# An S5 recurrence rewritten as a real scan in a turning frame, and a pause ahead of the scores of cached keys

## The chip, the core and the metric

The kernel runs on one core of a Trainium2 chip. The metric is the time of one execution in device microseconds. The engines are named as the profile names them: PE (TensorE; PEld is its loading of weights), DVE (VectorE), ACT (ScalarE), POOL (GpSimd) and SP (SyncE, which here issues nearly all DMAs). Each engine works through its own instructions strictly in the order in which they were written; a semaphore wait of one instruction holds all behind it on that engine.

## The reference

One inference step of a two-layer trunk for two groups of positions that share weights: a prompt of 256 frames and a running stream ("sample") of 32 frames with 512 cached keys. The width is 2048. Layer 0 is attention: 8 heads with a forget bias and 8 "differential" heads (two softmax maps each). Layer 1 is a diagonal complex state-space layer (S5): 128 groups of 16 channels with 64 complex states each. Cut to what the change touches:

```
# differential heads; k is the cached keys followed by the new ones
s = q @ k.T * scale + bias            # bias = -slope * distance
p = softmax(s1) - lam * softmax(s2)
# S5: abar = exp(dt * a), complex, one value for each (group, state)
bu      = einsum(u, bbar)             # complex input of each state
x[t]    = abar * x[t-1] + bu[t]       # x[-1] is zero (prompt) or the stream's state (sample)
y[t]    = Re(c @ x[t]) + d * u[t]
```

The outputs are the new residual streams of both groups, new cache rows, and the final states of both groups.

## The kernel before

All 288 positions (256 + 32) are processed at once, with features on the partitions. The weights stream from memory as tiles `w` of 1 MB through four slots (`wst`). Each quarter of a tile (128x512) is split into a rounded part `hi` (a CAST on ACT) and a rest `lo` (a subtraction on DVE), since one matmul takes reduced-precision operands; the activations are split likewise into `ah` and `al`. A 128x128 block of weights then costs three matmuls into `m`: `ah,hi`, `al,hi`, `ah,lo`. There are 8 `hi`/`lo` buffers (NQ). These m matmuls are the main stream, and a "job" of the main stream is 48 of them.

All else is side work, written as Python generators (`Tasks`): attention heads, the adaLN modulation (`mod_ps`), discretisation (`disc`), and the S5 stage. A planner (`Plan`) keeps a modelled clock for each engine while the program is built: a cost for every instruction, a "written" and "read" time for every region of a tile. After each main-stream block `Tasks.step` lets a side task go on when the planner's PE time has passed `plan.last`, the end of what that task last wrote; the words that a task yields (`"next dve"`, `"next soon"`, `"act"`) say which engine's backlog may hold it. So the order on all five engines is fixed at build time, out of estimated costs. Every engine call goes through the wrapper `Engine`, hence line L116 for all instructions in the profile: one goes by tile names.

`diff_sample(b, ck)` computes the sample group's scores of a pair of differential heads: it loads the bias `bi`, and then multiplies queries with the cached keys `CK` (`ck`, loaded by DMA CK<-in_kdT) into `Ss`, and with the new keys into `Ss2`.

In the S5 stage the position axis is cut into blocks of LC = 8; the state is carried from block to block, so there are JP = 32 steps for the prompt and 4 for the sample (NJ = 36; NX = 38 columns with the two starting states). The side tasks of the stage:
- `state_in` takes the four 512-wide groups of u (16 feature tiles, four at a time). When a group is done on the main stream it is written to memory (ud<-MX) and gathered back in another layout (MX<-ud, eight small DMAs). Matmuls `xin_ps` (16 units xin1 to xin16, four for a group of u) give the block inputs, and ACT copies them into X.
- `scan(g0)` runs the recurrence over blocks for 16 of the 64 group pairs at once, four times in all, one for each group of u. Before, it is a loop over the 32 steps, of four small instructions at first (prompt and sample together) and of three later (prompt alone), all on DVE, with tiles `t` and `rot`, the matrix of the eighth power of abar.
- `slices` (16 units y1 to y16): ACT copies the states into `Xm`, matmuls with a loaded tile `v` give `y_ps`, ACT copies them into `Yg`, and each four of them go to memory (yd<-Yg, eight small DMAs). The v tiles come through a ring of three.
- `inside` (16 units t1 to t16): the part within a block, matmuls t_ps with tiles `kb`.
- the gelus load yd back (yx<-yd), add it to MX on DVE, and take the ACT function (yx<-MX).

The four groups of u end after 192, 384, 576 and 768 m matmuls of this stage (counted from its first); the gates z follow.

Of the kernel before, what the change touches and what calls it, by code (L numbers as in the profile page):

```python
# [8 lines left out]
F32 = mybir.dt.float32  # L9
# [15 lines left out]
NJ = T // LC  # L25
# [70 lines left out]
class Engine:  # L96
# [38 lines left out]
    def cost(self, fn, out, ins, outs, k):  # L135
        p = self.plan
        n = 1
        for d in out.shape[1:]:
            n *= d
        if fn == "dma_start":  # L140
            t = max([p.when(p.written, a) for a in ins] + [p.at[self.name], p.base.get(out.tensor.name, 0.0)])
            p.at[self.name] = t + (0.45 if self.name != "pool" else 1.0)
            size = self.pieces(out, ins[0])
            if self.name == "act":
                end = t + 3.2 + 2 * size
            else:
                p.at["dma"] = max(p.at["dma"], t + 1.2) + size
                end = p.at["dma"] + 2.0
            p.note(p.written, out, end)
            for a in ins:  # L150
                p.note(p.read, a, end)
            p.last = max(p.last, end)
            return
        if self.name == "pe":
            r = ins[1] if len(ins) > 1 else ins[0]
            w = 1
            for d in r.shape[1:]:
                w *= d
            m = out.shape[0]
            c = 0.107 if fn != "matmul" else w * 0.00042 + 0.01 if r.dtype == F32R else max(w * 0.00042, 0.024) if m <= 32 \  # L160
                else max(w * 0.00168, m * 0.00167)
            c += 0.003
        elif self.name == "act":
            c = n * 0.000833 + 0.1 + (0.1 if len(outs) > 1 else 0)
        elif self.name == "dve":
            if fn == "tensor_reduce":
                n = ins[0].shape[1] * (ins[0].shape[2] if len(ins[0].shape) > 2 else 1)
            c = 0.07 + n * (0.0063 if fn == "reciprocal" else 0.00055 if fn in ("tensor_copy", "memset") or fn == "tensor_scalar" and len(ins) < 2 else 0.00105)
# [103 lines left out]
def build(tc, I, O):  # L272
# [8 lines left out]
    with ExitStack() as ctx:  # L281
# [23 lines left out]
        def TT(o, a, b, op, eng=dve):  # L305
            eng.tensor_tensor(o, a, b, op=op)
# [401 lines left out]
        def disc(V, rot, spt):  # L708
# [29 lines left out]
            yield  # L738
            TT(apr[:, :, 1], mg, s2, ALU.mult)
            TT(api[:, :, 1], mg, s1, ALU.mult)  # L740
            yield "next"
            for k in range(2, 9):
                p, q = k // 2, k - k // 2
# [4 lines left out]
                TT(s2, api[:, :, p], apr[:, :, q], ALU.mult)  # L748
                TT(api[:, :, k], s1, s2, ALU.add)
                yield "next"  # L750
            dve.tensor_copy(rot[:, :, 0:4:3], apr[:, :, 8:9].to_broadcast([128, 64, 2]))
            tsc(rot[:, :, 1], api[:, :, 8], -1.0)
            dve.tensor_copy(rot[:, :, 2], api[:, :, 8])
            TT(s1, ar, ar, ALU.mult)
            TT(s2, ai, ai, ALU.mult)
            TT(s1, s1, s2, ALU.add)
# [530 lines left out]
        def diff_sample(b, ck):  # L1287
            q, k = qkv["qd", b], qkv["kd", b]
            bi = sc.tile([128, PAST + TS], F32, tag="bias_s", name="bi")
            sp.dma_start(bi, I["biasS"][b])  # L1290
            nm = sc.tile([128, 2], F32, tag="nms", name="nms")
            sm = sc.tile([128, 2], F32, tag="sms", name="sms")
            zz = [sc.tile([128, PAST + TS], F32, tag="zs%d" % m, name="zs") for m in range(2)]
            for m in range(2):
                yield from room(2)
                S, S2 = take([128, PAST], "Ss"), take([128, TS], "Ss2")
                sample_scores(S, S2, q, k, ck, slice(64 * m, 64 * m + 64))
                if m:
# [24 lines left out]
            yield from sample_out(zz[0], "d", b, cv, scale)  # L1323
# [143 lines left out]
        rot1 = sp1.tile([128, 64, 4], F32, name="rot1")  # L1467
        sp.dma_start(rot1, rot_d)
        SZ = sp1.tile([128, KT, T], F32, name="SZ")
        X = sp1.tile([128, 64, 2, NX], F32, name="X")  # L1470
        dT = pload("dT", (128, KT))
        hbglu = pload("bgluT", (128, KT))
        tsc(hbglu, hbglu, 0.5)
# [111 lines left out]
        def state_in():  # L1585

            w1_ahead(0)
            for i in range(KT):
# [21 lines left out]
                x = X[:, 4 * i:4 * i + 4]  # L1610
# [8 lines left out]
            ready.add("w1_read")  # L1619
            yield  # L1620

        def scan(g0):
            n = 16
            Xh = X[:, g0:g0 + n]
            rot = rot1[:, g0:g0 + n, :]
            dve.memset(Xh[:, :, :, 0:1], 0.0)
            dve.tensor_copy(Xh[:, :, :, JP + 1], sfin[:, 1, g0:g0 + n, :])
            for j in range(JP):
                if j < NJ - JP:
                    cur = Xh[:, :, :, j:j + JP + 2:JP + 1]  # L1630
                    nxt = Xh[:, :, :, j + 1:j + JP + 3:JP + 1]
                    t = [sl.tile([128, n, 2, 2], F32, tag="t%d" % i, name="t") for i in range(2)]
                    TT(t[0], cur, rot[:, :, 0:1].unsqueeze(3).to_broadcast([128, n, 2, 2]), ALU.mult)
                    TT(t[1], cur[:, :, ::-1, :], rot[:, :, 1:3].unsqueeze(3).to_broadcast([128, n, 2, 2]), ALU.mult)
                    TT(nxt, nxt, t[0], ALU.add)
                    TT(nxt, nxt, t[1], ALU.add)
                else:
                    nxt = Xh[:, :, :, j + 1]
                    t = sl.tile([128, n, 2, 2], F32, tag="t%d" % (j % 2), name="t")
                    TT(t, Xh[:, :, :, j].unsqueeze(2).to_broadcast([128, n, 2, 2]),  # L1640
                       rot.rearrange("p g (o r) -> p g o r", o=2), ALU.mult)
                    TT(nxt, nxt, t[:, :, :, 0], ALU.add)
                    TT(nxt, nxt, t[:, :, :, 1], ALU.add)
                yield "next soon"
            dve.tensor_copy(sfin[:, 0, g0:g0 + n, :], Xh[:, :, :, JP])
            dve.tensor_copy(sfin[:, 1, g0:g0 + n, :], Xh[:, :, :, NX - 1])
# [6 lines left out]

        def v_load(i):
            if i < KT:
                vt[i] = sl.tile([128, 2, 4, 9, 16], F32, tag="v%d" % (i % 3), name="v2")
                sp.dma_start(vt[i].rearrange("p r g k c -> p r (g k c)"), v2_d[i])

        def kb_load(i):
# [4 lines left out]
        def slices():  # L1664

            Xm = sl.tile([128, 4, 2, 2, NX - 1], F32, name="Xm")
            pool.memset(Xm, 0.0)
            for i in range(3):
                v_load(i)
            for i in range(KT):  # L1670
                yield from wait(("x", i // 4))
# [1 line left out]
                if i % 4 == 0:  # L1673
                    Yg = sl.tile([128, 32, NJ], F32, tag="Yg", name="Yg")
                for e in range(2):
                    act.copy(Xm[64 * e:64 * e + 64, :, :, e, :], X[64 * e:64 * e + 64, 4 * i:4 * i + 4, :, 0:NX - 1])
                yield "act"
                yield from room()
                ps = take([128, 4, 2, NX - 1], "y_ps")
# [5 lines left out]
                act.copy(y[:, :, :, 0:JP], ps[:, :, :, 0:JP])  # L1685
                act.copy(y[:, :, :, JP:NJ], ps[:, :, :, JP + 1:NX - 1])
                give(ps)
                v_load(i + 3)
                if i % 4 == 3:
                    plan.last = plan.when(plan.written, Yg)  # L1690
                    yield "act"
# [133 lines left out]
        free = X.rearrange("p a r j -> p (a r j)")  # L1825
# [159 lines left out]
```

## Time and profile before

| | |
|---|---|
| runs shown | 1337.06 us median of 3 (1335.88 to 1342.54) |
| the profiled execution | 1335.96 us, of which its span is 1334.2 us |
| granted clock of TensorE, mean | 0.974 |
| PE busy | 1248.5 us, 94% |
| PEld, DVE, ACT busy | 1107.4, 922.8 and 593.8 us |
| DMA | 334.56 MB, mean 251 GB/s |

The columns of a timeline row are start (us), duration (us), engine, line, operation, tiles, shapes, count, and in brackets the idle time of the engine ahead of it with what ended it. A row of the windows has the stretch, its length, the busy time of PE, PEld, DVE, ACT and POOL with the number of instructions, then the granted clock (1.00 is full speed), the busy share of the DMA engines and the GB/s. A row of the waits has the engine and what it was about to do, what it waited for, the sum (us), the times and the longest.

### The profile page before, as it was taken

The numbers are of one execution on the slowest core, as the hardware profiler recorded it, in microseconds if no ns is written. First come the engines' busy times: TensorE is split into PE (matmuls) and PEld (weight loads), VectorE is DVE, ScalarE is ACT, GpSimd is POOL, SyncE is SP. The second block draws the span as 40 slices with busy tenths as digits, with TensorE's granted clock in tenths as the row PEclk, the third lists the DMA queues.
The fourth block names the chain that finished last, engine by engine and source line by source line (L and its number), as shares of the span: only waits on it lengthen the run. The fifth ranks groups of instructions, "written<-read, shape, count | busy, mean of one in ns | idle before, by whom it ended". The sixth has DMA issues, their size and how long they took to land.

```text
span 1334.2 us, 27951 instructions
## 1 busy us (share of the span) xinstructions
PE 1248.5 (94%) x11098; PEld 1107.4 (83%) x11098; DVE 922.8 (69%) x2210; ACT 593.8 (45%) x1394; POOL 31.1 (2%) x20
## 2 busy tenths in 40 slices
PE   5999899999999969999999999998879999999996
PEld 2798788888778858887889998897869999999895
DVE  5579987698887777887664873865749585455554
ACT  4534233344354524654643573242435684444441
POOL 0006000000000000000000000000000000000000
PEclk8999999999999979999999999998889999999998
DMA  9978687588989858988776396876657657677631
GB/s 356 370 294 335 225 306 260 190 296 336 323 284 356 310 201 290 324 302 311 275 253 228 133 362 168 195 220 176 161 162 187 189 184 267 236 273 269 228 123 71
DMA packets 114161, 334.56 MB, mean 251 GB/s; under 512 B 47696, under 2 KB 64096, under 8 KB 83312
## 3 DMA queue, kind: packets, MB, share of 16 engines
q1 hardware_dynamic: 101360, 303.14, 65.5%
q10 hardware_dynamic: 12672, 29.65, 6.1%
q8 instruction: 87, 1.43, 0.4%
q14 instruction: 42, 0.34, 0.1%
HBM read 297.69 MB, written 35.06 MB: 249 GB/s over the span
## 4 chain that ended last, share of the span: by engine, by line
issue 43%; PE 31%; DVE 12%; DMA 10%; ACT 3%; POOL 0%; ACTq 0%; SPq 0%; DVEq 0%; POOLq 0%
PE m L116 24%; DMA w<-in_w_in_att 4%; PE mod_ps L116 4%; DMA v_d<-v 3%; DVE lo L116 3%; DVE v L116 2%; DVE MX L116 1%; DMA w_d<-W 1%; DVE tmpv L116 1%; ACT hi L116 1%; DVE qkv L116 1%; DVE dtmp L116 1%; DVE ssq L116 1%; DMA CK<-in_kdT 1%; DVE al L116 1%
## 5 line engine op out<-in xcount | busy, mean ns | idle before, releaser
L116 PE MATMUL m<-ah,hi 128*128 128x288 f32 (+1 forms) x2304 | 712.6, 309 | 9.7 <-ACT hi L116 4.8
L116 PE MATMUL m<-ah,lo 128*128 128x288 f32 (+1 forms) x2304 | 686.5, 298 | 1.7 <-DVE lo L116 1.6
L116 PE MATMUL m<-al,hi 128*128 128x288 f32 (+1 forms) x2304 | 687.4, 298 | 0.0
L116 PEld LDWEIGHTS m<-ah,hi 128*128 128x128 f32 x2304 | 439.8, 191 | 69.5 <-issue 33.9
L116 ACT CAST hi<-w 128x512 fp32r<-128x512 f32 x552 | 322.5, 617 | 358.0 <-PE m L116 236.6
L116 DVE TENSOR_TENSOR lo<-w,hi 128x512 fp32r<-128x512 f32 x552 | 369.6, 687 | 144.9 <-ACT hi L116 142.4
L116 PEld LDWEIGHTS m<-ah,lo 128*128 128x128 f32 x2304 | 440.0, 191 | 3.1 <-DVE lo L116 3.0
L116 PEld LDWEIGHTS m<-al,hi 128*128 128x128 f32 x2304 | 440.4, 191 | 0.3
L116 PE MATMUL mod_ps<-w,cs 128*32 128x512 f32 x744 | 97.8, 620 | 12.6 <-DVE ssq L116 12.6
L116 DVE SCALAR_TENSOR_TENSOR qkv<-m,qkv 128x288 f32<-128x288 f32 x168 | 73.3, 454 | 26.0 <-PE m L116 25.8
L116 DVE TENSOR_TENSOR X<-X,t 128x32 f32<-128x32 f32 (+1 forms) x256 | 58.1, 227 | 8.3
L116 DVE TENSOR_TENSOR v<-pt,raw 128x512 f32<-128x512 f32 (+1 forms) x64 | 46.0, 719 | 22.1 <-DMA v_d<-v 18.8
L116 DVE SCALAR_TENSOR_TENSOR MX<-m,gate,MX 128x256 f32<-128x256 f32 x96 | 30.8, 363 | 31.2 <-PE m L116 31.1
L116 PEld LDWEIGHTS mod_ps<-w,cs 128*32 128x32 f32 x744 | 17.2, 110 | 38.2 <-issue 22.0
L116 PE MATMUL y_ps<-Xm,v 128*128 128x74 f32 x256 | 34.3, 292 | 13.0 <-ACT Xm L116 12.8
L116 DVE TENSOR_TENSOR tmpv<-pt,raw 128x512 f32<-128x512 f32 (+1 forms) x64 | 46.0, 718 | 0.0
L116 PEld LDWEIGHTS y_ps<-Xm,v 128*128 128x128 f32 x256 | 33.3, 209 | 13.9 <-ACT Xm L116 13.9
L116 ACT ACTIVATE yx<-MX 128x288 f32<-128x288 f32 (+1 forms) x38 | 18.8, 495 | 56.4 <-DVE MX L116 55.8
L116 PE MATMUL t_ps<-MX,kb 32*32 32x288 f32 (+7 forms) x1024 | 40.1, 306 | 2.8 <-DMA kb<-kb_d 2.8
L116 PEld LDWEIGHTS t_ps<-MX,kb 32*32 32x32 f32 x1024 | 28.7, 107 | 14.3 <-issue 4.4
L116 DVE SCALAR_TENSOR_TENSOR MX<-MX,c_dT,t_ps 128x288 f32<-128x288 f32 x16 | 8.2, 513 | 44.0 <-PE t_ps L116 44.0
L116 DVE TENSOR_TENSOR v<-v,tmpv 128x512 f32<-128x512 f32 (+1 forms) x48 | 34.3, 714 | 1.7
(225 smaller groups left out, 904.3 us busy)
## 6 DMA issues: line engine op xcount, KB each, us to landing
w<-in_w_mod SPq DMA_DIRECT2D x93, 1024.0 KB, 6.2
w<-in_w_in_att SPq DMA_DIRECT2D x40, 1024.0 KB, 7.7
w<-in_w_in_ssm SPq DMA_DIRECT2D x32, 1024.0 KB, 5.4
w<-in_w_wide SPq DMA_DIRECT2D x24, 1024.0 KB, 10.3
w<-in_w_out_att SPq DMA_DIRECT2D x16, 1024.0 KB, 6.9
w<-in_w_glu SPq DMA_DIRECT2D x14, 1024.0 KB, 5.1
w<-in_w_out_ssm SPq DMA_DIRECT2D x12, 1024.0 KB, 5.0
v_d<-v ACTq DMA_DIRECT2D x16, 576.0 KB, 7.8
```

What stands on the lines that cost most here:

```text
L116: return f(*a, **k)
```

## The change

Four things change.

1. Discretisation (`disc`): `rot` no longer holds the eighth power of abar as a matrix. It now holds the cosine and sine of eight times the angle (three rounds of angle doubling), and the eighth power of the magnitude. The planner gets a cost of its own for `tensor_tensor_scan`.
2. `diff_sample`: after its tiles are made, the task sets `plan.last` to the time at which the planner expects `ck` and `bi` to be there, and yields. So other work is put ahead of `Ss` until the planned PE time has reached that.
3. The S5 recurrence. A new task `turn_task` builds for each 16 group pairs the turns E[j] = (cos, sin) of j times the angle by doubling (w = 1, 2, 4, 8, 16: five rounds of four DVE instructions), and a table R of decays (an ACT copy). `scan` multiplies the inputs by the conjugate turn, runs the real and the imaginary part as one `tensor_tensor_scan` each (16 chains of 38 columns in a row, a decay of 0 at each start), and multiplies back. X gets the layout [part, group, column], so that a scan reads one contiguous row.
4. The ring of the v tiles has two slots in place of three (`v_load(i + 2)`).

The core of the diff:

```diff
@@ disc
+            for _ in range(3):
+                TT(n_, s1, s1, ALU.mult)
+                TT(th, s2, s1, ALU.mult)
+                TT(s2, s2, s2, ALU.mult)
+                TT(s2, s2, n_, ALU.subtract)
+                tsc(s1, th, 2.0)
+            dve.tensor_copy(rot[:, :, 0], s2)
+            dve.tensor_copy(rot[:, :, 1], s1)
+            TT(mg, mg, mg, ALU.mult)
+            TT(mg, mg, mg, ALU.mult)
+            TT(rot[:, :, 2], mg, mg, ALU.mult)
+            dve.memset(rot[:, :, 3:4], 0.0)
...
-            dve.tensor_copy(rot[:, :, 0:4:3], apr[:, :, 8:9].to_broadcast([128, 64, 2]))
-            tsc(rot[:, :, 1], api[:, :, 8], -1.0)
-            dve.tensor_copy(rot[:, :, 2], api[:, :, 8])
@@ diff_sample
+            plan.last = max(plan.when(plan.written, ck), plan.when(plan.written, bi))
+            yield
             for m in range(2):
                 yield from room(2)
@@ the S5 stage
-        X = sp1.tile([128, 64, 2, NX], F32, name="X")
+        X = sp1.tile([128, 2, 64, NX], F32, name="X")
...
+        def turn_task():
+            n = 16
+            for h in range(4):
+                yield from wait(*[("x", h - 1)] * (h > 0))
...
+                dve.tensor_copy(E[:, :, :, 1], rot[:, :, 0:2])
+                act.copy(R, rot[:, :, 2:3].to_broadcast([128, n, NX]))
+                dve.memset(R[:, :, 0:JP + 2:JP + 1], 0.0)
+                yield "next dve"
+                for w in (1, 2, 4, 8, 16):
...
+                    TT(t, a[:, :, ::-1, :], z, ALU.mult)
+                    TT(b, a, c, ALU.mult)
+                    TT(b[:, :, 0], b[:, :, 0], t[:, :, 0], ALU.subtract)
+                    TT(b[:, :, 1], b[:, :, 1], t[:, :, 1], ALU.add)
+                    yield "next dve"
+                dve.tensor_copy(E[:, :, :, JP + 1:NX], E[:, :, :, 0:NX - JP - 1])
@@ scan, inner part
-            for j in range(JP):
-                if j < NJ - JP:
...
-                    TT(t[0], cur, rot[:, :, 0:1].unsqueeze(3).to_broadcast([128, n, 2, 2]), ALU.mult)
-                    TT(t[1], cur[:, :, ::-1, :], rot[:, :, 1:3].unsqueeze(3).to_broadcast([128, n, 2, 2]), ALU.mult)
-                    TT(nxt, nxt, t[0], ALU.add)
-                    TT(nxt, nxt, t[1], ALU.add)
-                else:
...
-                yield "next soon"
+            for back in range(2):
+                for h in range(0, n, m):
...
+                    TT(t, Xh[:, ::-1], z, ALU.mult)
+                    TT(Xh, Xh, c, ALU.mult)
+                    yield "next soon"
+                    TT(Xh[:, 0], Xh[:, 0], t[:, 0], ALU.subtract if back else ALU.add)
+                    TT(Xh[:, 1], Xh[:, 1], t[:, 1], ALU.add if back else ALU.subtract)
+                    yield "next soon"
+                for ri in range(0 if back else 2):
+                    x = X[:, ri, g0:g0 + n, :].rearrange("p g j -> p (g j)")
+                    dve.tensor_tensor_scan(x, R.rearrange("p g j -> p (g j)"), x, 0.0, op0=ALU.mult, op1=ALU.add)
+                    yield "next soon"
@@ v ring
-                vt[i] = sl.tile([128, 2, 4, 9, 16], F32, tag="v%d" % (i % 3), name="v2")
+                vt[i] = sl.tile([128, 2, 4, 9, 16], F32, tag="v%d" % (i % 2), name="v2")
...
-                v_load(i + 3)
+                v_load(i + 2)
@@ start of the S5 stage
+        side.add(turn_task())
         side.add(state_in())
```

The order on the engines moves at many places. Three of them follow.

First, PE, at the first scores of the sample group's cached keys against the second pair of heads. Before:

```order
L116 MATMUL m<-ah,lo 128x288
L116 MATMUL S<-qkv 128x128
L116 MATMUL S<-qkv 128x256
L116 MATMUL Ss<-CK,MX 32x512 x4
L116 MATMUL Ss_5869<-qkv,MX 32x32 x4
L116 MATMUL m<-ah,hi 128x288
```

The same place on PE with the change:

```order
L116 MATMUL m<-ah,lo 128x288
L116 MATMUL S<-qkv 128x128
L116 MATMUL S<-qkv 128x256
L116 MATMUL m<-ah,hi 128x288
L116 MATMUL m<-al,hi 128x288
L116 MATMUL m<-ah,lo 128x288
```

Ss now comes 77 rows further on. Ahead of it stand 72 more m matmuls, one more pair of S, and two groups of mod_ps and one of k_ps. The position of its load (CK<-in_kdT) on SP, up to that point, is the same.

Second, DVE, as the S5 layer's activations are split (`al`), ahead of the first m matmuls of the stage. (`nrm` and `yx<-c_ident` belong to the norm, `turn` is E, `turn_t` its scratch tile.) Before:

```order
L116 TENSOR_TENSOR lo<-w,hi 128x512 x3
L116 SCALAR_TENSOR_TENSOR al<-MX,scl,ah 128x8x32
L116 SCALAR_TENSOR_TENSOR al<-MX,scl,ah 128x8x4
L116 TENSOR_TENSOR lo<-w,hi 128x512
L116 SCALAR_TENSOR_TENSOR al<-MX,scl,ah 128x8x32
L116 SCALAR_TENSOR_TENSOR al<-MX,scl,ah 128x8x4
```

With the change, from the same first row:

```order
L116 TENSOR_TENSOR lo<-w,hi 128x512 x3
L116 SCALAR_TENSOR_TENSOR al<-MX,scl,ah 128x8x32
L116 SCALAR_TENSOR_TENSOR al<-MX,scl,ah 128x8x4
L116 MEMSET turn 128x16 x2
L116 COPY turn<-rot_8970 128x32
L116 MEMSET decay 128x16x2
L116 TENSOR_TENSOR lo<-w,hi 128x512
L116 SCALAR_TENSOR_TENSOR al<-MX,scl,ah 128x8x32
L116 SCALAR_TENSOR_TENSOR al<-MX,scl,ah 128x8x4
L116 TENSOR_TENSOR turn_t<-turn 128x32
L116 TENSOR_TENSOR turn<-turn 128x32
L116 TENSOR_TENSOR turn<-turn,turn_t 128x16 x2
```

The first table of turns is built between the pieces of `al`, five rounds and a copy in all, where nothing stood before; the last and longest round stands between the first and the second piece of `al` of the third quarter of the activations (c = 2).

Third, SP, at the third group of u, its gather, and the first four slices' way out. Before:

```order
L116 DMA ud<-MX 128x4x288
L116 DMA v_11086<-v_d 128x1152
L116 DMA v_11143<-v_d 128x1152
L116 DMA w<-in_w_in_ssm 128x2048
L116 DMA MX<-ud 16x32x36 x8
L116 DMA yd<-Yg 16x32x36 x8
```

With the change:

```order
L116 DMA v_11012<-v_d 128x1152
L116 DMA ud<-MX 128x4x288
L116 DMA yd<-Yg 16x32x36 x8
L116 DMA w<-in_w_in_ssm 128x2048
L116 DMA MX<-ud 16x32x36 x8
```

The eight yd<-Yg moved from behind the gather to ahead of it, and ud<-MX now comes behind a v load that waits for slice y4. On ACT, in the same stage, a gelu's function yx<-MX, which waits for DVE and the load yx<-yd, stands ahead of the `Xm` copies of y10 before, and ahead of those of y9 with the change.

On PE the order of the units of the stage, by the number of m matmuls ahead of them, moves thus: y3 from 582 to 570, y4 from 600 to 582, xin9 from 648 to 720, xin12 from 684 to 762, y5 from 768 to 750, y8 from 828 to 792, xin13 from 846 to 804, y9 from 906 to 858, y12 from 990 to 960, y16 from 1200 to 1152; y1 stays at 534.

More of the change, by code (lines that the diff above doesn't have):

```diff
@@ L167, in cost @@
                 n = ins[0].shape[1] * (ins[0].shape[2] if len(ins[0].shape) > 2 else 1)
-            c = 0.07 + n * (0.0063 if fn == "reciprocal" else 0.00055 if fn in ("tensor_copy", "memset") or fn == "tensor_scalar" and len(ins) < 2 else 0.00105)
+            c = 0.07 + n * (0.0063 if fn == "reciprocal" else 0.0022 if fn == "tensor_tensor_scan" else 0.00055 if fn in ("tensor_copy", "memset") or fn == "tensor_scalar" and len(ins) < 2 else 0.00105)
         else:
@@ L1609, in state_in @@
                                ug[:, 8 * (i % 4) + 2 * g + e, :])
-                x = X[:, 4 * i:4 * i + 4]
+                x = X[:, :, 4 * i:4 * i + 4, :].rearrange("p r g j -> p g r j")
                 act.copy(x[:, :, :, 1:JP + 1], ps[:, :, :, 0:JP])
@@ L1620, in state_in @@
             yield
-        def scan(g0):
[L1623 to L1627, printed above, removed]
-            for j in range(JP):
-                if j < NJ - JP:
-                    cur = Xh[:, :, :, j:j + JP + 2:JP + 1]
-                    nxt = Xh[:, :, :, j + 1:j + JP + 3:JP + 1]
-                    t = [sl.tile([128, n, 2, 2], F32, tag="t%d" % i, name="t") for i in range(2)]
-                    TT(t[0], cur, rot[:, :, 0:1].unsqueeze(3).to_broadcast([128, n, 2, 2]), ALU.mult)
-                    TT(t[1], cur[:, :, ::-1, :], rot[:, :, 1:3].unsqueeze(3).to_broadcast([128, n, 2, 2]), ALU.mult)
-                    TT(nxt, nxt, t[0], ALU.add)
-                    TT(nxt, nxt, t[1], ALU.add)
-                else:
[L1638 to L1643, printed above, removed]
-                yield "next soon"
-            dve.tensor_copy(sfin[:, 0, g0:g0 + n, :], Xh[:, :, :, JP])
-            dve.tensor_copy(sfin[:, 1, g0:g0 + n, :], Xh[:, :, :, NX - 1])
@@ new lines, in build @@
+        turns = {}
+        def turn_task():
+            n = 16
+            for h in range(4):
+                yield from wait(*[("x", h - 1)] * (h > 0))
+                E = sl.tile([128, n, 2, NX], F32, tag="turn", name="turn")
+                R = sl.tile([128, n, NX], F32, tag="decay", name="decay")
+                turns[h] = E, R
+                rot = rot1[:, n * h:n * h + n, :]
+                dve.memset(E[:, :, 0, 0:1], 1.0)
+                dve.memset(E[:, :, 1, 0:1], 0.0)
+                dve.tensor_copy(E[:, :, :, 1], rot[:, :, 0:2])
[3 more added lines that the diff above has]
+                for w in (1, 2, 4, 8, 16):
+                    a, b = E[:, :, :, 1:w + 1], E[:, :, :, w + 1:2 * w + 1]
+                    c, z = (E[:, :, i, w:w + 1].unsqueeze(2).to_broadcast([128, n, 2, w]) for i in range(2))
+                    t = turn_tmp(2 * n * w).rearrange("p (g r j) -> p g r j", g=n, r=2)
+                    TT(t, a[:, :, ::-1, :], z, ALU.mult)
[4 more added lines that the diff above has]
+                dve.tensor_copy(E[:, :, :, JP + 1:NX], E[:, :, :, 0:NX - JP - 1])
+                ready.add(("turn", h))
+                yield
@@ new lines, in turn_tmp @@
+        def turn_tmp(size):
+            return sl.tile([128, 16 * NX], F32, tag="turn_t", name="turn_t")[:, 0:size]
+        def scan(g0):
+            n, m = 16, 8
+            Xq = X[:, :, g0:g0 + n, :]
+            yield from wait(("turn", g0 // n))
+            E, R = turns.pop(g0 // n)
+            dve.memset(Xq[:, :, :, 0:1], 0.0)
+            dve.tensor_copy(Xq[:, :, :, JP + 1], sfin[:, 1, g0:g0 + n, :].rearrange("p g r -> p r g"))
+            for back in range(2):
+                for h in range(0, n, m):
+                    Xh = Xq[:, :, h:h + m, :]
+                    c, z = (E[:, h:h + m, i].unsqueeze(1).to_broadcast([128, 2, m, NX]) for i in range(2))
+                    t = turn_tmp(2 * m * NX).rearrange("p (r g j) -> p r g j", r=2, g=m)
+                    TT(t, Xh[:, ::-1], z, ALU.mult)
[8 more added lines that the diff above has]
+                    yield "next soon"
+            dve.tensor_copy(sfin[:, 0, g0:g0 + n, :], Xq[:, :, :, JP].rearrange("p r g -> p g r"))
+            dve.tensor_copy(sfin[:, 1, g0:g0 + n, :], Xq[:, :, :, NX - 1].rearrange("p r g -> p g r"))
@@ L1667, in slices @@
             pool.memset(Xm, 0.0)
-            for i in range(3):
+            for i in range(2):
                 v_load(i)
@@ L1675, in slices @@
                 for e in range(2):
-                    act.copy(Xm[64 * e:64 * e + 64, :, :, e, :], X[64 * e:64 * e + 64, 4 * i:4 * i + 4, :, 0:NX - 1])
+                    act.copy(Xm[64 * e:64 * e + 64, :, :, e, :], X[64 * e:64 * e + 64, :, 4 * i:4 * i + 4, 0:NX - 1].rearrange("p r g j -> p g r j"))
                 yield "act"
@@ L1824, in build @@
         st_free.append(NST)
-        free = X.rearrange("p a r j -> p (a r j)")
+        free = X.rearrange("p r a j -> p (r a j)")
         more.update(tiles={NST: lambda: free[:, 0:2048].rearrange("p (k n) -> p k n", k=4)}, until=len(jobs))
```

## The prediction

> **What bounds the kernel now.** I read the page's header and busy times first, then the waits of PE.
>
> ```profile
> span 1334.2 us, 27951 instructions
> PE 1248.5 (94%) x11098; PEld 1107.4 (83%) x11098; DVE 922.8 (69%) x2210; ACT 593.8 (45%) x1394; POOL 31.1 (2%) x20
> PE y_ps L116 <- ACT Xm L116: 12.8, 3, 8.1
> PE Ss L116 <- DMA CK<-in_kdT: 10.1, 1, 10.1
> PE xin_ps L116 <- DMA yd<-Yg: 3.4, 1, 3.4
> ```
>
> PE is the bound: 1248.5 of 1334.2 us. The change neither adds nor removes a matmul, so it can win only from the 85.7 us in which PE idles and from time at a lowered clock. DVE at 69% is no bound over the whole; saving its time counts only where PE waits for it. The sum below is made against the profiled 1335.96 us, 1.1 us under the median of 1337.06.
>
> The windows around the wait for CK show that a wait costs more than itself:
>
> ```profile
> 472.00:482.00 10.00, 0.00 (x0) 0.00 (x0) 2.92 (x5) 1.04 (x3) 0.00 (x0) 0.68 0.78 267
> 482.00:487.00 5.00, 4.89 (x28) 3.59 (x29) 2.87 (x6) 0.00 (x0) 0.00 (x0) 0.50 0.02 5
> 487.00:492.00 5.00, 5.00 (x39) 3.65 (x40) 4.97 (x13) 1.87 (x4) 0.00 (x0) 0.78 0.37 129
> ```
>
> PE does nothing from 472 to 482, and then runs at clock 0.50 for 5 us and at 0.78 for another 5: 2.5 + 1.1 = 3.6 us more.
>
> The S5 stage has eight holes on PE. These are the rows that end them, with the stage as one window:
>
> ```profile
> 811.26 1.13 PE L116 MATMUL xin_ps<-MX,W1r 128*64 128x36 f32 x32 [1.30 <-DMA kb<-kb_d]
> 857.87 1.13 PE L116 MATMUL xin_ps<-MX,SZ 128*64 128x36 f32 x32 [1.14 <-issue]
> 905.93 1.47 PE L116 MATMUL xin_ps<-MX,SZ 128*64 128x36 f32 x23 [3.40 <-DMA yd<-Yg]
> 915.52 1.64 PE L116 MATMUL t_ps<-MX,kb 32*32 32x288 f32 x13 [2.75 <-DMA kb<-kb_d]
> 940.01 1.35 PE L116 MATMUL y_ps<-Xm,v 128*128 128x74 f32 x5 [3.16 <-ACT Xm L116]
> 967.39 1.13 PE L116 MATMUL xin_ps<-MX,W1r 128*64 128x36 f32 x32 [1.40 <-DMA MX<-ud]
> 993.30 1.56 PE L116 MATMUL y_ps<-Xm,v 128*128 128x74 f32 x6 [8.12 <-ACT Xm L116]
> 1034.84 1.45 PE L116 MATMUL y_ps<-Xm,v 128*128 128x74 f32 x11 [1.57 <-ACT Xm L116]
> 780.00:1060.00 280.00, 257.05 (x2961) 240.43 (x2960) 180.47 (x585) 119.68 (x310) 0.00 (x0) 0.95 0.68 192
> ```
>
> They sum to 22.8 us. A mean clock of 0.95 over 280 us is 14 us lost; I put 3 of them inside the holes themselves, which leaves 11 in work that ran slowly. The stage so loses about 34 us, and DVE is busy in 64% of it: late hand-overs, not a full engine.
>
> **The pause ahead of Ss.** It removes the wait for CK if the work now ahead of Ss fills it. That work is 72 m matmuls, 2 mod_ps groups, k_ps and S. Rows of PE, DVE and SP say whether it is fed:
>
> ```profile
> 460.15 0.38 PE L116 MATMUL m<-ah,hi 128*128 128x288 f32 x1
> 462.73 1.06 PE L116 MATMUL mod_ps<-w,cs 128*32 128x512 f32 x8
> 471.11 1.28 DVE L116 TENSOR_TENSOR lo<-w,hi 128x512 fp32r<-128x512 f32 x2
> 478.89 0.43 DVE L116 TENSOR_TENSOR Fm<-Fb,c 128x256 f32<-128x256 f32 x1 [4.37 <-DMA Fb<-Fp_d]
> 472.42 0.33 SPq L116 DMA_DIRECT2D w<-in_w_mod  x1
> ```
>
> Between the first row and mod_ps lie 18 m matmuls in 2.58 us, 0.14 us each; 72 of them are 10 us, and mod_ps and k_ps add one to two. That is 11 to 12 us, against a wait of 10.1: it fits. What could be late next is the split of the weights, since DVE sat behind Fm until 478.89. Counted in the order, DVE has made the `lo` of 204 quarters by the row at 471.11 and PE has used 198.5, so 66 of the 72 matmuls are ready at once; one further `lo` now stands ahead of Fm, and three behind it. The w_mod of 472.42 is wanted by the second mod_ps group some 10 us later; the CK load issued right behind it landed after 9, so that is close, 0 to 2 us. Bounds: all of the wait and its clock, 13.7; or the weight stream late by the same DMA backlog, which gives back about 10 of it. I take 13, since the rows show the split ahead of need. The sample group's later steps move by some 12 us; they have no reader on PE for a long while.
>
> On such clock losses the Trainium skill ("TensorE: Matmul & The Clock Gate", the table of states in "What's actually happening") says that PE falls to half clock after about 3.4 us of idleness and recovers after about 3.4 us of work, 1.7 us lost to a hole. The rows above show 3.6 us lost behind this hole, and at 915.52 a hole of 2.75 us among small matmuls; by the page's figure the pause would be worth 11.8 us and the sum below would come out some 2 us higher. I go by the rows.
>
> **Discretisation.** It gains 21 small DVE instructions and loses 3, each 128x64, in one block at 150 to 160 us:
>
> ```profile
> 140.00:160.00 20.00, 17.84 (x156) 13.60 (x156) 19.32 (x63) 5.05 (x9) 0.00 (x0) 1.00 0.50 178
> L116 DVE TENSOR_TENSOR dtmp<-dtmp 128x64 f32<-128x64 f32 x4 | 0.9, 225 | 0.1
> ```
>
> 18 x 0.22 is 4.0 us. DVE is busy for 19.32 of 20 there and PE idles 2.16, so DVE sets the pace and little hides it: 2 to 4, I take +3.
>
> **The scan itself.** Removed and added, by duration:
>
> ```profile
> L116 DVE TENSOR_TENSOR X<-X,t 128x32 f32<-128x32 f32 (+1 forms) x256 | 58.1, 227 | 8.3
> L116 DVE TENSOR_TENSOR t<-X,rot 128x64 f32<-128x64 f32 x144 | 33.2, 240 | 1.5
> L116 DVE TENSOR_TENSOR lo<-w,hi 128x512 fp32r<-128x512 f32 x552 | 369.6, 687 | 144.9 <-ACT hi L116 142.4
> L116 DVE TENSOR_TENSOR MX<-MX,yx 128x576 f32<-128x576 f32 x8 | 6.0, 754 | 8.1 <-DMA yx<-yd 8.1
> L116 DVE TENSOR_TENSOR_SCAN f_Fs<-f_one,f_lfs 8x544 f32<-8x544 f32 x1 | 1.3, 1253 | 0.0
> L116 DVE TENSOR_TENSOR_SCAN f_Fp<-f_one,f_lfp 8x256 f32<-8x256 f32 x1 | 0.7, 678 | 0.0
> ```
>
> Out go 58.1 + 33.2 = 91.3 us. From the two scans, (1253 - 678)/288 = 2.0 ns an element, so one of 608 takes 1.38 us. From 225 ns at 64, 687 at 512 and 754 at 576, a multiply of 608 takes 0.79 and one of 304 about 0.47. A call of `scan` is then 8 x 0.79 + 8 x 0.47 + 2 x 1.38 and copies, 13.5 us; the turns are rounds of about 0.75, 0.85, 1.05, 1.45 and 2.2 with copies and memsets, 7 us. Four times 20.5 is 82: DVE gains 9 us in all, on an engine that is not the bound. What changes is how early a slice's states are there, and through the planner the order.
>
> **The first turns, among `al`.** They have no predecessor, so the planner puts them early:
>
> ```profile
> 777.87 0.64 DVE L116 SCALAR_TENSOR_TENSOR al<-MX,scl,ah 128x256 fp32r<-128x256 f32 x2
> 775.00:780.00 5.00, 5.00 (x40) 5.00 (x39) 5.00 (x15) 4.49 (x14) 0.00 (x0) 1.00 1.06 381
> ```
>
> DVE is busy for all of 775 to 780 as PE is, and `al` is made piece by piece shortly before PE wants it. Some 6.5 us of turns go ahead of the third quarter's second `al` piece, which on the rows' pace has about 3 us in hand; 3 to 4 us of stall and a little clock, between 0 (if all of it slips into DVE's idle time behind, 785 on) and 8. I take +5.
>
> **What happens to the eight holes.** t12, y5 and y10 (2.75, 3.16, 8.12) lose their cause as they stood: kb loads and Xm come sooner against PE in the new order. New waits appear:
>
> ```profile
> 793.53 1.40 SPq L116 DMA_DIRECT2D ud<-MX  x1
> 881.32 0.39 SPq L116 DMA_DIRECT2D ud<-MX  x1
> 889.82 11.77 SPq L116 DMA_DIRECT2D MX<-ud  x8
> 901.68 6.54 SPq L116 DMA_DIRECT2D yd<-Yg  x8
> 945.06 0.38 SPq L116 DMA_DIRECT2D ud<-MX  x1
> v<-v_d SPq DMA_DIRECT2D x13, 576.0 KB, 6.6
> 986.76 1.51 DVE L116 TENSOR_TENSOR MX<-MX,yx 128x576 f32<-128x576 f32 x2 [7.80 <-DMA yx<-yd]
> 987.55 1.43 ACT L116 ACTIVATE yx<-MX 128x576 f32<-128x576 f32 x2 [8.12 <-DVE MX L116]
> ```
>
> From ud<-MX to the first matmul on its gather it took 17.7 us (793.53 to 811.26), 24.6 (881.32 to 905.93) and 22.3 (945.06 to 967.39).
> - xin1 and xin5: PE has about as long as before; 0.5 each.
> - xin9: 720 in place of 648 gives PE 138 matmuls (18.4 us) and a t unit after ud. The yd<-Yg now stand ahead of the gather, but they issue while ud still flies. 20 to 24 against 21: 0 to 4, I take 2.
> - xin13: 42 matmuls sooner, so PE has about 17.4 us where the gather takes 17.7 to 22.3. 0 to 7, I take 5.
> - y9: on ACT its Xm copy stands behind a gelu's yx<-MX, which waits on DVE for yx<-yd; this is what the last two rows show for y10 before, 8.12 us. The yd go out sooner against PE than then, so between 0 and 8 I take 3.5.
> - v ring of two: a v tile is issued after y(i) and needed at y(i+2). Where slices follow closely (y2 to y4, y6 to y8) that is 24 m matmuls, 3.4 us, a slice (16 matmuls at 1.45 us for 11, as at 1034.84, 2.1 us) and at times an xin unit, 5.5 to 6.6, against a landing of 6.6. 0 to 3 in all; I take 1.
>
> That is 12.5 us of holes, and at the rate of before (11 to 22.8) some 5 of clock behind them: 17.5 in place of 34, so -16.5.
>
> **The sum.** -13 + 3 + 5 - 16.5 = -21.5; 1336 - 21.5 is 1314.5 for the profiled execution, near 1316 as a median.
>
> **The rivals.**
> - *The hole moves (pause gives back 10).* The DMA share is 0.78 in the hole, so PE may meet late weights once it does not stop. For it: w_mod's closeness. Against it: PE shows no wait there for a weight DMA, and the two windows behind the hole have shares of 0.02 and 0.37, idle time that the stream can use. It gives 1326.
> - *Only the pause counts.* The holes of the S5 stage are set by ud, yd and the gathers, whose path the scan doesn't touch; the new order only shifts where PE meets them. For it: five of the eight rows name a DMA or issue. Against it: two of the three largest name Xm. -13 + 3 + 5 is -5, so 1332.
> - *Slower: the small DMAs on SP become the bound.* Four times 8 gathers and 8 yd writes pass in order on one queue, at 6.5 to 11.8 us for eight. If the yd written ahead of the gather are not covered by ud's flight, xin9 comes 8.5 + 6.5 + 11.8 us after ud, 27, and if the backlog carries on to xin13 and y9, the stalls are some 6, 14 and 14 with half clock behind each, about 46 in place of 34 while the pause gives only 4. -4 + 3 + 5 + 12 is +16; it decides once the stage's stalls exceed 30. 1350.
> - *The scan instruction is slower* over 128 partitions than the rows on 8: at twice the time it adds 11 us to DVE, 2.8 to each scan; mostly hidden, it adds 2 to 4 to the sum, and lies within the likeliest case.
> - *No effect:* the pause lands where CK is late all the same, and the stage refills. 1337.
>
> **Chances.** The sum as it stands 0.62 (its own range 1303 to 1326), the hole moves 0.12, only the pause 0.13, slower 0.08, no effect 0.05. A measurement of this kernel can tell about 0.5% from no change, 6.7 us: faster is below 1330.4, slower above 1343.7. Faster takes the first two and a part of the third, 0.77; the same 0.14; slower 0.09. The range reaches from a stage that loses nearly all its holes (1300) to the third case's upper side (1336).
>
> **What would show it.** The wait of Ss for CK is gone or below 2 us, and the clock between 470 and 500 is 1.00. Near 780 there is a new PE wait for `al` of 3 to 6 us. xin13 and y9 are the stage's largest holes. DVE's busy time falls by 5 to 10 us and scans take 1.4 us each. It is wrong if PE waits for `hi` or `lo` where CK was, if y4 or y8 wait for v by several us, or if the stage's clock stays at 0.95.

## The result, and the profile after

The changed kernel takes 1318.8 us (median of 4, 1315.82 to 1324.34) against 1336.47 for the kernel before on the same chip. The ratio is 0.9872, with a 95% interval of 0.9834 to 0.9910; once more, on another chip, it was 0.9883 (0.9853 to 0.9912). That is 16 to 17 us less, where the prediction had 1316 us and a sum of -21.5. One execution of a later kernel (each scan twice, unknown to the planner) took 1984 us at a granted clock of 0.56, and its ratio leaves that one out.

The profiled execution has a span of 1322.4 us, and is the slowest of the four. Its first lines, and some of its waits of PE:

```profile
span 1322.4 us, 27713 instructions
PE 1245.6 (94%) x11098; PEld 1106.7 (84%) x11098; DVE 912.3 (69%) x2000; ACT 595.2 (45%) x1398; POOL 31.0 (2%) x20
PE xin_ps L116 <- DMA MX<-ud: 6.3, 1, 6.3
PE m L116 <- DVE qkv L116: 6.0, 3, 3.5
PE m L116 <- DVE lo L116: 5.4, 5, 3.5
PE m L116 <- DVE al L116: 3.6, 1, 3.6
PE y_ps L116 <- ACT Xm L116: 2.6, 1, 2.6
PE Ss L116 <- DMA CK<-in_kdT: 1.9, 1, 1.9
```

The wait of 10.1 us for CK is gone (the 1.9 is at 609 us, for the second group of heads), and of the 12.8 us for Xm 2.6 are left. New are 6.3 for a gather (1.4 before) and 3.6 for `al`, and there is more for qkv and lo. DVE's busy time fell by 10.5 us (922.8 to 912.3).

To see where the time went, both timelines of PE were cut at the same work: the time at which the n-th m matmul starts (there are 6912 in each). The differences to the profile of the kernel before, in us, are these, with the changed kernel in its first profile and in a second one:

| m matmuls | place | predicted | first | second |
|---|---|---|---|---|
| to 850 | start, discretisation | +3 | +4.9 | +3.7 |
| 850 to 2250 | attention, orders alike | 0 | +7.9 | +3.1 |
| 2250 to 2400 | the wait for CK | -13 | -16.0 | -15.6 |
| 2400 to 3900 | rest of attention | 0 | +2.2 | +2.2 |
| 3900 to 4000 | `al` of the S5 layer | +5 | +6.3 | +6.5 |
| 4000 to 6000 | S5 stage | -16.5 | -17.1 | -18.1 |
| all | | -21.5 | -11.8 | -18.2 |

Without the second row the stretches come to -19.7 and -21.3, near the prediction's sum. The second row, attention with the orders alike, is the rest: the prediction put it at nothing, and it lost 7.9 and 3.1.

The windows of the changed kernel at the place where PE stood still for 10 us before (CK is issued at 484.75 here), and the row of Ss:

```profile
480.00:490.00 10.00, 10.00 (x83) 8.33 (x83) 9.78 (x18) 3.54 (x8) 0.00 (x0) 1.00 0.64 228
490.00:500.00 10.00, 10.00 (x82) 8.18 (x82) 7.18 (x18) 3.45 (x11) 0.00 (x0) 1.00 1.01 407
496.81 1.06 PE L116 MATMUL Ss<-CK,MX 64*32 64x512 f32 x8
```

PE is busy throughout at clock 1.00, and Ss starts without a wait, 12.1 us after its load was issued. The gap has been filled, and the slow 10 us behind it are gone too.

In the S5 stage and just ahead of it, these rows end the holes of over 1 us that are left, with the window behind the first:

```profile
779.44 0.61 PE L116 MATMUL m<-al,hi 128*128 128x290 f32 x1 [3.60 <-DVE al L116]
780.00:785.00 5.00, 5.00 (x23) 5.00 (x22) 4.96 (x16) 1.96 (x6) 0.00 (x0) 0.51 0.98 359
818.00 1.13 PE L116 MATMUL xin_ps<-MX,W1r 128*64 128x36 f32 x32 [2.77 <-DMA kb<-kb_d]
920.42 1.93 PE L116 MATMUL xin_ps<-MX,SZ 128*64 128x36 f32 x32 [6.34 <-DMA MX<-ud]
978.53 1.79 PE L116 MATMUL y_ps<-Xm,v 128*128 128x74 f32 x11 [2.62 <-ACT Xm L116]
```

Eight holes have become three, 22.8 us have become 11.7. Some of the new instructions on DVE, by form:

```profile
L116 DVE TENSOR_TENSOR X<-X,turn_t 128x304 f32<-128x304 f32 x32 | 13.7, 469 | 0.1
L116 DVE TENSOR_TENSOR X<-X,turn 128x608 f32<-128x608 f32 x16 | 12.7, 793 | 0.6
L116 DVE TENSOR_TENSOR_SCAN X<-decay,X 128x608 f32<-128x608 f32 x8 | 11.2, 1416 | 0.0
```

### The profile page after: what moved, and what is told of

It reads as the page before. It is cut to its first block, busy times and chain, and to the rows that moved or that the text cites. A ratio compares the mean times of both kernels' runs of the same rounds, so it can differ in the third digit from the quotient of the medians.

```text
span 1322.4 us, 27713 instructions
## 1 busy us (share of the span) xinstructions
PE 1245.6 (94%) x11098; PEld 1106.7 (84%) x11098; DVE 912.3 (69%) x2000; ACT 595.2 (45%) x1398; POOL 31.0 (2%) x20
## 4 chain that ended last, share of the span: by engine, by line
issue 48%; PE 25%; DMA 14%; DVE 10%; ACT 1%; SPq 1%; ACTq 0%; POOL 0%; POOLq 0%; DVEq 0%
PE m L116 19%; DMA w<-in_w_in_att 5%; DMA v_d<-v 5%; PE mod_ps L116 3%; DVE v L116 3%; DVE lo L116 2%; DVE tmpv L116 1%; DMA w_d<-W 1%; DMA w<-in_w_wide 1%; DVE dtmp L116 1%; DMA w<-in_w_mod 1%; DVE MX L116 1%; ACT hi L116 1%; SPq L116 1%; PE w_ps L116 1%
## 5 line engine op out<-in xcount | busy, mean ns | idle before, releaser
L116 PE MATMUL w_ps<-c_ident,v 128*128 128x128 f32 x128 | 20.4, 283 | 10.4 <-ACT hi L116 2.1
## 6 DMA issues: line engine op xcount, KB each, us to landing
w<-in_w_wide SPq DMA_DIRECT2D x24, 1024.0 KB, 10.5
```

The lines of the kernel that those rows point to most:

```text
L116: return f(*a, **k)
```

## The experiments

Ratios are to the kernel before, run on the same chip, with 95% intervals. "Stage" is the stretch from 4000 to 6000 m matmuls in the profile, against before.

**The pause alone.** The edit, put into the kernel before:

```diff
+            plan.last = max(plan.when(plan.written, ck), plan.when(plan.written, bi))
+            yield
```

> The kernel before with the pause ahead of the cached keys' scores and nothing else. Theory A (the parts add up: pause -16, discretisation +4, first turns +6, S5 stage -17 us by the profiles' milestones): about 1336 - 14 to -16 = 1321 us, the wait of Ss for CK gone or below 2 us, S5 stage with its old holes. Rival B (the pause only moves its wait; the S5 stage makes the gain): within 5 us of before, a new wait for weights or for lo between 480 and 700 us.

1324.47 us, ratio 0.9900 (0.9876 to 0.9923): -13.4 us. The stretch of the CK wait is 14.9 shorter, and its profile has no wait for CK; 550 to 620 us give back some 3. The stage is as before (+2). Theory A, at the small end of what it gave.

**All but the pause.** The same two lines taken out of the changed kernel.

> The changed kernel without the pause. Theory A: the rest of the change is worth -17 + 4 + 6 = -7 us against the kernel before, about 1329 to 1331 us, with the wait of Ss for CK back at about 10 us. Rival B: it keeps nearly all of the gain, 1320 us or less.

1330.17 us, ratio 0.9949 (0.9928 to 0.9971): -6.8 us, as theory A has it. The stage is 13.0 shorter here; whether that differs from the 17 to 18 with the pause, one profile can't tell. The wait is back:

```profile
PE Ss L116 <- DMA CK<-in_kdT: 10.2, 1, 10.2
```

The two halves make -20, the whole -16 to -17, each uncertain by 3 to 5: the parts add up about as well as can be measured.

**The first turns later.**

```diff
-                yield from wait(*[("x", h - 1)] * (h > 0))
+                yield from wait(("x", h - 1) if h else ("h1", 3))
```

> The changed kernel, with the first table of turns begun only after the last piece of al is written. Theory A (7 us of turns ahead of al make PE wait 3.6 us near 780 us and run slowly behind it, 6 us in all): 5 to 7 us faster than the changed kernel, no PE wait for al. Rival C (PE would have waited there anyway, for lo or for weights): same as the changed kernel within 2 us. Rival D: the first scan is late by the moved 7 us and y1 waits for it, so the gain is given back.

1310.43 us, ratio 0.9800 (0.9766 to 0.9834), against 0.9883 for the changed kernel: -11 us by the ratios, uncertain by 6. In the profile the stretch at `al` costs 0.0 in place of +6.5, no PE wait names `al`, and the stage keeps its gain (-17.8). Theory A; the first scan has time enough to do without the early start.

**The changed kernel once more.**

> The changed kernel once more, on the same chip as the three others. In its first profile PE lost 8 us between 305 and 376 us, where both kernels have the same order of instructions. Theory E (that is the landing time of a DMA, v_d<-v, which differs from one execution to the next): the loss against the kernel before in that stretch is not the same again, 0 to 5 us. Rival F (it follows from the 4 us that the discretisation adds ahead of it): 8 us again.

1320.62 us, ratio 0.9883. Between 305 and 376 us it lost nothing (-0.6 from 1500 to 1900 m matmuls, in place of +7.9). In the first profile DVE there waited for a transfer. This is the row in the kernel before, and then the same row in the changed one, with PE's wait that followed:

```profile
309.71 0.69 DVE L116 TENSOR_TENSOR v<-pt,raw 128x512 f32<-128x512 f32 x1 [1.57 <-DMA v_d<-v]
```

```profile
318.36 0.69 DVE L116 TENSOR_TENSOR v<-pt,raw 128x512 f32<-128x512 f32 x1 [5.67 <-DMA v_d<-v]
321.04 0.61 PE L116 MATMUL m<-ah,lo 128*128 128x288 f32 x1 [3.48 <-DVE lo L116]
```

Theory E for that stretch: v_d<-v, issued at 307.45, held its buffer until 318.36, 10.9 us (301.99 to 309.71 before, 7.7). Some 5 of the 7.9 us are lost at this place, the rest behind it. But 3.7 us were lost between 1900 and 2250 instead. Over all runs of this study the stretch from 1500 to 1900 cost 0 (-0.2 to +0.5) in the three other profiles with the old discretisation; with the new one it cost -0.6 to +2.2 in six and +7 to +8 in two, and with the doublings on POOL +3.5 in one and -0.3 in the other. So the order does not fix the loss; whether the change makes it likelier stays open.

**The order without the DVE work.** Twice the recurrence's multiplications, additions and scans, and the building of the turns, are left out while the planner still charges for them, so that the order on PE, ACT and SP stays what it was: once in the kernel before, once in the changed one. The states are then only the blocks' inputs. The diff is of the first; the second does the same to its instructions.

```diff
+            def TT(o, a, b, op):
+                dve.cost("tensor_tensor", o, [x for x in (a, b) if x is not o], [o], {})
```

> The kernel before with the recurrence's 400 multiplications and additions left out (the states are then only the blocks' inputs), while the planner still charges for them, so that the order of all other instructions on every engine is that of before. DVE loses 91 us of work in the S5 stage and the states are there at once. Theory G (the stage's gain of 17 us in the changed kernel comes from the order, in which slices and gathers stand elsewhere, and from a shorter wait, hardly from DVE's 9 us): the holes whose cause is Xm (3.2, 8.1, 1.6 us) lose the part that came from DVE, those that name DMAs stay, 0 to 10 us faster than before although ten times as much DVE work is gone as in the change. Rival H (DVE time is what the stage lacks): 20 us faster or more, and the stage's holes gone.

> The changed kernel with the turns, the multiplications and the scans left out (the states are the blocks' inputs), while the planner still charges for them: the order of all else is that of the changed kernel. With the kernel before, the same without its recurrence, and the changed kernel this makes a square of two orders by with and without the DVE work; between 4000 and 6000 m matmuls the three lose 0 (before), -14 (without recurrence) and -17 to -18 us (changed) against before. Theory P (the order and the DVE work each count for about half of the stage's gain): -24 to -28 us in this stretch, and with the first turns gone 1302 to 1306 us. Rival Q (the order alone; DVE work is hidden in the new one): -17 to -20 us, about 1312. Rival R (what holds the stage are the transfers, the same for both orders once DVE is free): -14 to -16 us here, no better than the old order.

In the order of before: 1320.84 us, ratio 0.9880 (0.9851 to 0.9909), stage -14.2. That is 16 us, between the two theories. Three holes of over 1 us remain in the stage; the two long ones name the cause that they had:

```profile
910.84 1.60 PE L116 MATMUL t_ps<-MX,kb 32*32 32x288 f32 x12 [5.98 <-DMA kb<-kb_d]
980.44 1.77 PE L116 MATMUL y_ps<-Xm,v 128*128 128x74 f32 x7 [7.60 <-ACT Xm L116]
```

In the order of the changed kernel: 1308.65 us, ratio 0.9772 (0.9748 to 0.9795), stage -17.9, the same as with all of its DVE work. The two longest holes stay as well:

```profile
904.59 1.68 PE L116 MATMUL xin_ps<-MX,SZ 128*64 128x36 f32 x27 [6.85 <-DMA MX<-ud]
962.78 2.56 PE L116 MATMUL y_ps<-Xm,v 128*128 128x74 f32 x16 [2.83 <-ACT Xm L116]
```

So Q's number for the stage: the square reads 0 and -14 with and without the work in the old order, -17 to -18 and -18 in the new one. In the old order the recurrence cost 14 us; in the new one its successor costs PE nothing that one profile can show. Without any recurrence the new order is still 4 us better than the old, in one profile of each. That the order alone makes the gain, as Q says, is not shown: either the work left out in the old order, or the new order, brings most of it, and the two together hardly more. (By the ratios the kernel is 4 us below that with late turns, within the uncertainty.)

**Each scan twice.** Once behind the planner's back, and once with its knowledge; the diff is of the first.

```diff
                     dve.tensor_tensor_scan(x, R..., x, 0.0, op0=ALU.mult, op1=ALU.add)
+                    nc.vector.tensor_tensor_scan(x, R..., x, 0.0, op0=ALU.mult, op1=ALU.add)
```

> The changed kernel with each of its eight scan instructions carried out twice, unknown to the planner, so the order is the same but for these; the second pass changes the states. Adds eight times 1.4 us, 11 us, to DVE in the S5 stage, a little more than the 9 us that the change saved there. Theory G: 0 to 4 us slower than the changed kernel, from scans that end 2.8 us later. Rival H: 9 us slower or more.

> The changed kernel with each scan instruction carried out twice, as in the run before of that kind, but the planner is told of the second pass, so it sets the order anew around 11 us more of DVE work. Unknown to it, the same work cost 8 us of the run (0.9945 of before against 0.9883), with waits for lo of up to 2.4 us; leaving out all of the recurrence's DVE work in the changed order won nothing in the stage. Theory U (the order is exact to a microsecond or two, and work that it does not know of makes lo late; known work is moved to where DVE has time): within 4 us of the changed kernel, ratio to before 0.985 to 0.991, and no more PE waits for lo than in the changed kernel (1.8 us). Rival V (DVE has no time left in the stage, known or not): 8 us slower than the changed kernel again, ratio about 0.994.

Unknown: ratio 0.9945 (0.9924 to 0.9965), 8 us slower than the changed kernel for 11 us of work, uncertain by 5, between G's 4 and H's 9. In the profile the stage is at -3 in place of -17 to -18, so 14 to 15 us are lost there; that is H's side. PE now waits where the extra scans stand among the splits of weights:

```profile
843.89 0.40 PE L116 MATMUL m<-ah,lo 128*128 128x290 f32 x1 [2.36 <-DVE lo L116]
904.72 0.40 PE L116 MATMUL m<-ah,lo 128*128 128x290 f32 x1 [2.06 <-DVE lo L116]
```

Known: ratio 0.9988 (0.9959 to 1.0016), 14 us slower than the changed kernel, stage +5. My theory U fell. V's time is passed, but V's cause is not what the profile shows either: the planner made another order, with eight yd<-Yg between ud and the gather of the fourth group of u in place of the third, and PE's two longest waits in the stage are these:

```profile
981.85 1.40 PE L116 MATMUL xin_ps<-MX,W1r 128*64 128x36 f32 x22 [9.09 <-DMA MX<-ud]
1047.21 0.61 PE L116 MATMUL m<-ah,hi 128*128 128x290 f32 x1 [5.89 <-ACT h1sh L116]
```

How much of that is the planner's order and how much the work itself can be told in part: unknown, the work moved the stage by 14 to 15 us, and known, work and new order together by 22 to 23, in one profile each.

**The writes of the slices on POOL.**

```diff
-                        sp.dma_start(dst[s], Yg[16 * s:16 * s + 16])
+                        pool.dma_start(dst[s], Yg[16 * s:16 * s + 16])
```

> The kernel with late turns, with the 32 writes yd<-Yg issued by POOL in place of SP. Theory I (xin9 waits 6.2 to 6.6 us since eight yd<-Yg stand ahead of the eight gathers MX<-ud on SP and hold them): the wait at xin9 is below 3 us, and 3 to 8 us are gained against late turns alone. Rival J (the gathers are slow because yd, v and the weights share the DMA engines with them, whoever issues): the wait stays at 5 us or more. Rival K: POOL issues its writes so slowly that yx<-yd and the last slices come late, and the kernel is slower.

> The kernel before with the 32 writes yd<-Yg issued by POOL in place of SP, and nothing else. Theory S (the writes on SP hold the gathers and the gelus' loads behind them in the old order too, so the old holes at xin9 of 3.4 us and y10 of 8.1 us come from there): 5 to 12 us faster than before, y10's wait below 4 us. Rival T (in the old order the recurrence is what makes the slices late): within 4 us of before.

With late turns: 1300.35 us, ratio 0.9733 (0.9698 to 0.9768), some 9 us below late turns alone, uncertain by 6 to 7 (stage -26.9 in place of -17.8). The planner made another order here, on PE too, so this is not the price of the queue alone. The third group's transfers on SP in the changed kernel come first, with what SP waited for between 890 and 920 and the load that it names. Behind them is the same place with the writes on POOL, with the wait at xin9:

```profile
893.06 0.43 SPq L116 DMA_DIRECT2D ud<-MX  x1
893.58 7.86 SPq L116 DMA_DIRECT2D yd<-Yg  x8
902.01 14.76 SPq L116 DMA_DIRECT2D MX<-ud  x8
SPq L116 <- DMA SZ<-w_d: 9.1, 1, 9.1
910.80 0.33 ACTq L116 DMA_DIRECT2D SZ<-w_d  x1
```

```profile
876.17 0.43 SPq L116 DMA_DIRECT2D ud<-MX  x1
876.60 5.17 POOL L116 DMA_DIRECT2D yd<-Yg  x8 [116.27 <-ACT Yg L116]
883.98 10.36 SPq L116 DMA_DIRECT2D MX<-ud  x8
899.42 1.13 PE L116 MATMUL xin_ps<-MX,SZ 128*64 128x36 f32 x32 [1.41 <-issue]
```

The gather begins 7.8 us after ud in place of 9.0, and is issued in 10.4 us in place of 14.8. Theory I's forecast came true, but not its reason. In the changed kernel three of the eight gathers go out by 905.2, and the other five from 914.35 on. In between SP waits for SZ<-w_d, a load for the matmuls xin_ps that ACT issued at 910.80 and that landed at 914.33. In the trace the transfers of SP and ACT take eight completion semaphores in turn (counters that tell of a landing), and each waits until the one that had its semaphore before has landed; SZ<-w_d took its turn among the eight yd<-Yg, and the fourth gather got the same semaphore. The writes of POOL have eight semaphores of their own, so the turns fall otherwise, and that hold is gone. It is there, with 8.1 to 12.1 us, in all seven profiles in which the eight writes stand on SP between ud and the gather of the third group, and the gather's issue takes 14.2 to 17.5 us in them. The 9.1 us of wait at xin13 with the scans doubled and known has a hold of 7.4 us by SZ<-w_d ahead of it.

In the kernel before, the same edit gives 0.9976 (0.9954 to 0.9997), -3 us: y10's wait of 8.1 is gone as S had it, but xin9 now waits 7.9 us, and the sum is T's. The order on PE is that of before here. POOL's writes now go out beside the gather, in whose issue no semaphore holds SP for long, and it takes 18.2 us (11.8 before):

```profile
891.55 5.15 POOL L116 DMA_DIRECT2D yd<-Yg  x8 [121.03 <-ACT Yg L116]
891.81 18.19 SPq L116 DMA_DIRECT2D MX<-ud  x8
912.68 1.61 PE L116 MATMUL xin_ps<-MX,SZ 128*64 128x36 f32 x26 [7.92 <-DMA kb<-kb_d]
```

So another queue for the writes is no gain by itself. That the writes slow the gathers whoever issues them, rival J, fits these rows, but no run separates it.

**The discretisation's doublings on POOL**, with late turns (`eng=pool` for the 18 instructions and the memset, other scratch for the powers after them):

> The kernel with late turns, with the angle doublings, copies and squarings of the discretisation (18 instructions of 128x64 and a memset) on POOL in place of DVE. Theory L (they cost PE the wait of 3.5 us for DVE's qkv near 138 us, and 1 to 5 us of the run): that wait falls below 1 us, 1 to 4 us faster than late turns alone. Rival M (DVE is full there anyway, and the work after it is only moved): the same within 1 us.

1311.62 us, ratio 0.9801 (0.9774 to 0.9829): the same as late turns. At its place the wait of 3.5 us is split up:

```profile
136.14 0.37 PE L116 MATMUL m<-ah,hi 128*128 128x288 f32 x1 [1.21 <-DVE qkv L116]
138.76 0.40 PE L116 MATMUL m<-ah,hi 128*128 128x288 f32 x1 [0.79 <-DVE qkv L116]
```

From 600 to 850 m matmuls, where the discretisation stands, it loses 0.4 against before, and late turns 2.7. That the time is the same all the same goes with another 6.7 us that its profile lost between 1500 and 2250 (late turns: 3.6): M by the time, L by the place, though the longest wait there is still 1.2.

**All three together.**

> The changed kernel with late turns, yd<-Yg issued by POOL, and the angle doublings of the discretisation on POOL. If the parts add up: late turns 1310, less 9 to 10 for the writes, less 0 to 2 for the discretisation, 1298 to 1301 us; no wait over 3 us in the S5 stage.

1298.49 us (1295.99 to 1303.27), ratio 0.9699 (0.9674 to 0.9725): 40 us below the kernel before, and 23 to 25 below the changed one. The longest wait in the stage is 2.8 us.

## Why the prediction was right, step by step

- *The pause*: -13 was taken, -14.6 to -16.0 measured at its place in the ten profiles that have it, and 2 to 4 given back between 2400 and 3900 m matmuls, where the second group of heads waits for zs and, in some profiles, for its CK load. That return wasn't in the sum, and is not the pause's for certain, since this stretch moves by -1.4 to +1.5 in the profiles without it; the rival that all of it returns is excluded by the pause alone. The clock loss behind the hole was real: it went with the hole.
- *The clock behind a hole*: at `al`, 3.60 us of idleness were followed by 5 us at 0.51, 2.5 us more. The Trainium skill ("TensorE: Matmul & The Clock Gate", the table of states in "What's actually happening") has full clock back after at least one busy window of about 3.4 us. One window at half clock, the prediction's 1.7 us, is thus the least, and by that estimate this place would have cost 5.3; it cost 6.3 and 6.5, and the measurement decides.
- *Discretisation*: +3; from 600 to 850 m matmuls the eight profiles that have it on DVE lose 2.7 to 4.1, and the two with it on POOL 0.4.
- *The first turns among `al`*: +5, with 3 to 4 of stall; 3.60 of stall and 6.3 to 6.5 in all. Undone, they are gone.
- *DVE's work*: a scan of 608 elements was put at 1.38 us and takes 1.416 (the x8 row above); 0.79 and 0.47 for the multiplications are 0.793 and 0.469. That the scan instruction is slow on 128 partitions is excluded.
- *The eight holes*: -16.5 in sum, -17 to -18 measured, but with its terms wrong in both directions. xin13 was put at 5 and waits 0: its first matmul starts 18.2 us after ud (937.47 to 955.66) and finds the gather there, which was issued in 4.8 us (8.9 before). y9 was put at 3.5 and waits 2.6 (3.1 in the second profile), for the reason given, as the rows of ACT below show: yx<-MX waits 6.62 us for DVE ahead of its Xm. xin9 was put at 2 and waits 6.2 to 6.6. The step "they issue while ud still flies" held: the gather begins 9.0 us after ud, 8.5 before. What failed is that the gather behind them was taken to go out as before; it takes 14.8 us in place of 11.8, and 9.1 of these are the hold by SZ<-w_d, which the prediction did not see. xin1 waits 0 to 2.8 in place of 0.5. The ring of two v tiles, put at 1, shows no wait of over 1 us in the changed kernel; it was not tried apart. The granted clock from 780 to 1060 is 0.97 and 0.98 in the two profiles, 0.95 before. Wrong terms of opposite sign made a right sum, so the stage's number was partly luck. The rows of ACT ahead of y9, in the first profile:

```profile
976.05 0.68 ACT L116 ACTIVATE yx<-MX 128x576 f32<-128x576 f32 x1 [6.62 <-DVE MX L116]
977.57 0.91 ACT L116 COPY Xm<-X 64x296 f32<-64x296 f32 x2
```

- *The rival "only the pause counts"* is excluded by the kernel without the pause (-6.8 us with some +8 from turns and discretisation in it). *The slower rival* did not occur in the changed kernel. Its first number did: xin9 comes 27.4 us after ud (893.06 to 920.42) where it had 27, and waits its 6. But the writes were covered by ud's flight; the hold by SZ<-w_d made the number, and no backlog went on to xin13 and y9.
- *That the saving of 9 us on DVE is not the gain* is borne out by the stage, which gained 17 to 18, but "an engine that is not the bound" was too simple: 11 us more on DVE, unknown to the planner, cost 8 us. DVE has time in the stage, though perhaps not at the places where scans and splits stand close.

What stays open, beside the write of v: how much of the stage's gain is owed to the new scan's shorter chain, and how much to the order that the planner happened to make of its costs. The new scan with the old order was not tried, since the planner sets the order by its instructions. How much the queue alone is worth in the writes' move to POOL stays open too, since the planner's order moved with it.

## What to carry to other kernels

Price a wait together with the slow clock behind it, and fill it with work whose inputs are already there; the order shows this, by counting what has been made and what has been used. When a faster instruction sequence goes into a kernel whose order is planned from costs, look at what the planner then puts ahead of what, on the DMA-issuing queue above all. Look at what that queue waits for as well: here a load on another engine, which shared a semaphore with a gather, held the queue for 9 us. Table-building work with no predecessor should get a start condition, or it goes where its engine is already the tight one.

## What the runs showed of the hardware that I had not expected

The issue of eight gathers of 72 KB on SP took 14.2 to 17.5 us in seven profiles, 8.1 to 12.1 of them a wait for the landing of a load that ACT had issued and that had the same completion semaphore. With the writes ahead of them on POOL's queue the issue took 10.4 us in one order, and 18.2 in another. And one write of v to memory held its buffer for 10.9 us in one execution and 7.7 in another, at the same place; PE lost some 5 us there and 7.9 in the whole stretch.
